# Sums of weights made by the transfers: 24 quads of a blocked fp32 kernel, and a third block carried through DRAM

## The chip, the cores and the metric

The kernel runs on one core of a Trainium2 chip. The metric is the device time of one launch in microseconds. The engines are named as in the profile: PE (TensorE matmuls), PEld (TensorE weight loads), DVE (VectorE), ACT (ScalarE), POOL (GpSimd), SP (SyncE, which issues most DMAs).

## The reference

One transformer-like layer on 256 tokens of width 2048, all in fp32: a gated feed-forward, a mixer and a second feed-forward, each behind a norm, added to the residual.

```python
def _swiglu(x, w_gate, w_up, w_down):
    return (jax.nn.silu(x @ w_gate) * (x @ w_up)) @ w_down

def _hybrid_mixer(u, w_in, ...):
    p = u @ w_in
    z_a, z_b, g_a, g_b = jnp.split(p, IN_SPLITS, axis=-1)
    y_a = _rwkv7_branch(z_a, ...) @ w_proj_a
    y_b = _pool_branch(z_b, pool_w, pool_scale) @ w_proj_b
    m = jax.nn.sigmoid(g_a) * y_a + jax.nn.sigmoid(g_b) * y_b
    return m @ w_out

h = x
f = _swiglu(_rmsnorm(h, ln_ffn1_pre), ffn1_gate, ffn1_up, ffn1_down)    # D_FF = 5632
h = h + 0.5 * _rmsnorm(f, ln_ffn1_post)
h = h + _rmsnorm(_hybrid_mixer(_rmsnorm(h, ln_mix_pre), ...), ln_mix_post)
f = _swiglu(_rmsnorm(h, ln_ffn2_pre), ffn2_gate, ffn2_up, ffn2_down)
h = h + 0.5 * _rmsnorm(f, ln_ffn2_post)
```

The RWKV branch is a recurrence over the 256 tokens in 16 heads; the pool branch takes running means. Nearly all arithmetic is in the products with the weights.

## The kernel before, in words

**Products in three passes.** A weight tile of 128 rows by 512 columns, two of them side by side, arrives in a buffer `w` (tag `w32`, five buffers of 128x1024). ScalarE copies it to a rounded type as `wH`, VectorE subtracts that from the original and gives the remainder `wL` (`split`). The activations have been split in the same way into `xH` and `xL`, transposed, so that a row block of 128 features is a stationary operand. `mm3` then issues three matmuls: high by high, high by low, low by high. A plain `pair` takes two row blocks k and k+1 for both halves of the tokens: 12 matmuls of 512 columns.

**Quads.** A `Columns` object treats two columns of 512 side by side: `f` and `l` (gate and up, or two neighbouring columns of one weight). For a quad, two row blocks k and k+1 of both columns are multiplied by a scheme with seven products in place of eight, in the manner of Strassen and Winograd. It needs sums of the activations (`sums`, kept in `sm`) and sums of the four weight tiles, made on VectorE: `t13` (128x1024: two first sums), then two further sums of 512 columns. `early` and `late` are the form in gate blocks and `quad` that in down and output columns. `join` and `merge` put the product banks together.

**Stages.** Each feed-forward has eleven gate blocks of 512 columns (`GATE1`, `GATE2`: how many quads each has; the early part of a block's quads runs inside the block before it), then `down` for the columns 0 and 1, and again for 2 and 3 (`DOWN1`, `DOWN2`: ten quads in each of the two, and where they start). The mixer's columns of `w_in` go in an order written out (`MIX_ORDER`), then come `w_proj_a` in four columns and `w_out` by `down` with three quads each time (`OUT_QUADS`: number, first, step).

**Turning blocks.** A result block [tokens, features] that feeds the next product must be transposed. There are two ways. `transpose_split` lets TensorE transpose it (four `tr` matmuls for each half of the tokens) and splits it out of PSUM. `carry` lets VectorE transpose blocks of 32x32 (`turned`, tile `T`), stores the result to DRAM (`cx<-T`) and fetches it back in four pieces in the right order (`x<-cx`). In the mixer the blocks c of the gated mix (`sga`) below `MIX_DMA` are carried, the others go through TensorE. `carry` also leaves in `raws` a way to get the block for the activation sums: here a second fetch.

**Order.** The program is recorded first. A planner (`Plan`) simulates it with costs and due times, and writes out one fixed order for each engine. For a transfer it takes bytes by `RATE` (335 bytes per ns) after 1900 ns, then `LAND` (1800 ns) and `CARRY` (1200 ns) where it depends on another transfer. Units `u` (36 buffers of 128x1024) hold everything else; spare ones are lent to `w32`, `wH` and `wL`.

Of the kernel before, what the change touches and what calls it, by code (L numbers as in the profile page):

```python
# [12 lines left out]
F32 = mybir.dt.float32  # L13
# [6 lines left out]
P = 128  # L20
# [27 lines left out]
EASE = 2.0  # L48
GATE1 = [0, 0, 3, 4, 4, 4, 4, 4, 4, 4, 4]
GATE2 = [0, 0, 3, 4, 4, 4, 4, 4, 4, 4, 4]  # L50
OUT_QUADS = ((3, 2, 1.0), (3, 1, 1.0))
DOWN1 = ((10, 1, 2.0), (10, 1, 1.3))
DOWN2 = ((10, 1, 2.0), (10, 1, 1.3))
SCRATCH = 1024
SPARE = 1
SPARE2 = 4
HOLD = 3e5
MIX_DMA = 2
Z_DMA = "l0 k0 v0 r0 k1 v1 r1"
POOL_DMA = [True, True]  # L60
MIX_ORDER = "B0 S l0 k0 p0+p1 r0 m0 m1 v0 m2 c0 B1 m3 k1 b0 b1 v1 r1 c1 B2 b2 B3 b3 A0 A1 A2 A3"
# [38 lines left out]
RATE = 335.0  # L100
LANES = 8
CARRY = 1200.0
SWITCH = 100.0
RUN = 16
COLD = 4800.0
# [6 lines left out]
KEPT = 4  # L112
# [3 lines left out]
class Plan:  # L116
# [155 lines left out]
    def deadlines(s):  # L272
        for o in s.ops:
            for p in o.preds:
                s.ops[p].succs.append(o)
        soon = {}
        for o in s.ops:
            if o.stream == "chain":
                soon[o.i] = max([soon[q] + s.ops[q].dur + SYNC for q in o.preds if q in soon
                                 and s.ops[q].nom == o.nom] or [0.0])  # L280
        idx, tip, run = {}, {}, []
        for o in s.ops:
            g = max([idx.get(q, -1) if s.ops[q].eng == "PE" else tip[q] for q in o.preds]
                    or [-1])
            tip[o.i] = g
            o.run = None
            if o.eng != "PE" or o.stream != "chain":
                continue
            idx[o.i] = len(idx)
            far = max([tip[q] for q in o.preds if s.ops[q].eng != "PE"] or [-1])  # L290
            if not run or run[-1].cfg != o.cfg or far >= idx[run[0].i] or len(run) == RUN \
                    or run[-1].psum[0].kind != o.psum[0].kind:
                run = []
            run.append(o)
            o.run = run
        for o in reversed(s.ops):
            d = o.nom + (0.0 if o.eng == "PE" else o.lag) + soon.get(o.i, 0.0) * EASE
            for x in o.succs:
                if o.eng == "PE" and x.eng == "PE":
                    continue  # L300
                e = x.dl - o.dur - SYNC - (2500 if o.nbytes else 0)
                if e < d:
                    d = e
            o.dl = d

    def simulate(s):
# [66 lines left out]
        def go(o):  # L373
# [22 lines left out]
            if o.nbytes:  # L396
                dma = max(now + 1900, dma) + o.dur
                o.end = dma + LAND
                if any(ops[q].nbytes for q in o.preds):
                    o.end += CARRY  # L400
                if e != "POOL":
                    lanes.append(o.end)
                    heapq.heappush(events, (o.end, next(rel), None))
            else:
                o.end = now + dur
# [125 lines left out]
class Block:  # L531
# [166 lines left out]
    def sums(s, x, out):  # L698

        nc = s.nc  # L700
        V = nc.vector
        fl = lambda t: t.rearrange("p a b t -> p (a b t)")
        (a11, a21), (a12, a22) = [[x[:, :, b, h] for h in range(2)] for b in range(2)]
        f = s.unit((P, 4, 2, P), F32, "sf")
        g = f if len(x.shape) < 6 else f.rearrange("p m a (i t) -> p m a i t", i=4)
        V.tensor_tensor(out=g[:, 0], in0=a21, in1=a22, op=ALU.add)
        V.tensor_tensor(out=g[:, 1], in0=g[:, 0], in1=a11, op=ALU.subtract)
        nc.scalar.mul(f[:, 0], f[:, 0], -1.0)
        V.tensor_tensor(out=g[:, 2], in0=a11, in1=a21, op=ALU.subtract)
        V.tensor_tensor(out=g[:, 3], in0=a12, in1=g[:, 1], op=ALU.subtract)  # L710
        fH, fL = [s.unit((P, 4, 2, P), F32R, n_) for n_ in ("sH", "sL")]
        s.split(fl(f), fl(fH), fl(fL))
        for i in range(2):
            out.append([(fH[:, m, i], fL[:, m, i]) for m in range(4)])
# [110 lines left out]
                in_=d.rearrange("(i s) (q c) -> q s i c", s=32, q=4)[q])  # L825
        return x

    def carry(s, T1, T, raws, j=None):
        x, d = s.carry_raw(T1)
        view = lambda t: t.rearrange("p (i a b h t) -> p a b h i t", i=4, a=2, b=2, h=2)  # L830
        if j is None:
            j = len(T)
            T.extend(s.new_T(1) if j < KEPT else [None])

        def parts():
            if T[j] is None:
                T[j], = s.new_T(1)
            H, L = [t.rearrange("p k (h c) -> p (k h) c", h=2)
                    .rearrange("p m (i t) -> p i m t", i=4) for t in T[j]]
            s.split(x.rearrange("p (i m t) -> p i m t", i=4, t=32), H, L)  # L840
        if T[j] is None:
            s.later[j] = parts
            raws.append(lambda: view(x))
        else:
            parts()
            raws.append(lambda: view(s.fetch(d, 1024, 4)))

    def sumsq(s, src, acc):
        s.nc.scalar.activation(out=s.rtmp("junk").bitcast(mybir.dt.bfloat16), in_=src,
# [17 lines left out]
class Columns:  # L867

    def __init__(s, blk, wf, cf, wl, cl, at, KT, sm, quads, bank, apart=None):
        s.b, s.wf, s.cf, s.wl, s.cl, s.at, s.KT, s.sm = blk, wf, cf, wl, cl, at, KT, sm  # L870
        s.quads, s.new, s.apart = quads, bank, apart
        n = len(quads)
        s.rest = [k for k in range(0, KT, 2) if k not in quads]
        std = KT - 2 * n
        s.left = dict(f0=std + n, f1=std, l0=std + n, l1=std + n)
        if apart:
            s.left.update(p1=n, p5=n, p6=n, p7=n)
        else:
            s.left.update(l0=std + 2 * n, f0=std + 2 * n, l1=std + 2 * n, f1=std + n)
        s.banks, s.t4 = {}, {}  # L880
# [13 lines left out]
    def pair(s, k, b):  # L894
        w, c0 = (s.wf, s.cf) if b == "f" else (s.wl, s.cl)
        for i, wH, wL in s.b.load_w(w, k, 2, c0, 512):
            for h in range(2):
                s.mul(f"{b}{h}", s.rows(i, h), (wH, wL))

    def early(s, k):  # L900
        q = s.b
        V = q.nc.vector
        va, vb = q.raw4(k, s.wf, s.cf, s.wl, s.cl)
        t13 = q.unit((P, 2, 512), F32, "t13")
        V.tensor_tensor(out=t13, in0=va, in1=vb[:, :1].to_broadcast([P, 2, 512]),
                        op=ALU.subtract)
        V.tensor_tensor(out=va[:, 1], in0=va[:, 0], in1=t13[:, 1], op=ALU.add)
        i = s.quads.index(k)
        if i % 2 == 0:
            s.t4[i] = q.unit((P, 2, 512), F32, "t4")  # L910
        V.tensor_tensor(out=s.t4[i - i % 2][:, i % 2], in0=vb[:, 1], in1=va[:, 1],
                        op=ALU.subtract)
        b11, t2 = q.halves(va)
        t1, t3 = q.halves(t13)
        S_ = s.sm[k // 2]
        end = k == s.quads[-1]
        s.mul("l0", s.rows(k, 0), b11, end)
        s.mul("f1", S_[1], t2, end)
        s.mul("f0", S_[0], t1, end)
        s.mul("l1", S_[2], t3, end)  # L920
# [14 lines left out]
    def join(s):  # L935
# [4 lines left out]
        A.copy(p5, b["f0"])  # L940
        V.tensor_tensor(out=b["f1"], in0=b["f1"], in1=u0, op=ALU.add)
        A.copy(s2, b["f1"])
        V.tensor_tensor(out=b["f0"], in0=b["f0"], in1=s2, op=ALU.add)
        V.tensor_tensor(out=b["l1"], in0=b["l1"], in1=s2, op=ALU.add)
        V.tensor_tensor(out=b["f1"], in0=b["l1"], in1=p5, op=ALU.add)

    def quad(s, k):
        q = s.b
        V = q.nc.vector
        va, vb = q.raw4(k, s.wf, s.cf, s.wl, s.cl)  # L950
        t13 = q.unit((P, 2, 512), F32, "t13")
        V.tensor_tensor(out=t13, in0=va, in1=vb[:, :1].to_broadcast([P, 2, 512]),
                        op=ALU.subtract)
        b11, b22 = q.halves(va)
        V.tensor_tensor(out=vb[:, 0], in0=va[:, 0], in1=t13[:, 1], op=ALU.add)
        t4 = q.tmp("t4")
        V.tensor_tensor(out=t4, in0=vb[:, 1], in1=vb[:, 0], op=ALU.subtract)
        t1, t3 = q.halves(t13)
        t2, b21 = q.halves(vb)
        h4 = q.unit((P, 2, 512), F32R, "h4")  # L960
# [12 lines left out]
    def merge(s):  # L973
# [4 lines left out]
        A.copy(u[0], b["p1"])  # L978
        add(u[1], b["p6"], u[0])
        add(u[2], b["p7"], u[1])  # L980
        add(u[1], b["p5"], u[1])
        add(u[3], b["p5"], u[2])
        s.u = dict(l0=u[0], l1=u[2], f0=u[1], f1=u[3])

    def plus(s, c):
# [6 lines left out]
class Kernel(Block):  # L992
# [31 lines left out]
    def ffn(s, wg, wu, wd, uT, rs, gpost, resid, emit, reload, quads, downs, xs=None):  # L1024
# [39 lines left out]
        for b in range(1, nb):  # L1064
            jobs[b] = Columns(s, wg, b * 512, wu, b * 512, s.T_at(nT) if b > 1 else at, NKD,
                              su, [2 * i for i in range(quads[b])],
                              s.psum if b % 2 else s.bank)
        for b in range(1, nb):
            J = jobs[b]
            while s.after and b == 3:  # L1070
# [6 lines left out]
        def late_T(k):  # L1077
            if hT[k // 4] is None:
                s.later[k // 4]()
            return at_h(k)  # L1080
        s.down(wd, late_T, NKF, s.post(gpost, 0.5, resid, emit, reload, xs is None), raws,
               downs, 4 * KEPT)

    def spread(s, rs, out):
        for h in range(2):
# [25 lines left out]
                s.sums(x.rearrange("p (a b) (h t) -> p a b h t", a=2, h=2), su)  # L1111
        return nT

    def down(s, wd, at, KT, ev, raws, plan, q0=0):
        sm = {}
        for c, (nq, first, step) in ((0, plan[0]), (2, plan[1])):
            J = Columns(s, wd, c * 512, wd, c * 512 + 512, at, KT, sm,
                        [q0 + 2 * i for i in range(nq)], s.bank, s.psum)
            quads = list(J.quads)
            tail = J.rest[-min(TRAIL, KT - 2 * nq) // 2:] if c else []  # L1120

            def col(b):
# [285 lines left out]
    def mixer(s, prm, uT, rs, resid, emit, gpost, reload):  # L1408
# [125 lines left out]
        sx = []  # L1534

        def sums_x():
            for i in range(MIX_SUMS):
                x = s.unit((P, 4, S), F32, "sx")
                uH, uL = [t.rearrange("p k t -> p (k t)").bitcast(F32) for t in uT[i]]
# [60 lines left out]
        for c in range(4):  # L1600
            s.gemm_tok(prm["w_proj_a"], c * 512, at_a, NKW, ev_pa(c))
        s.plan.lend = "O" in MIX_LEND
        s.down(prm["w_out"], s.T_at(mT), NKD, s.post(gpost, 1.0, resid, emit, reload), raws,
               OUT_QUADS)
        s.plan.lend = False

    def pool_window(s, win, zs, mxT):
# [538 lines left out]
```

## Time and profile before

| what | value |
|---|---|
| median of 3 runs | 1989.6 us (1989.53 to 1990.06) |
| profiled execution | 1989.87 us, span 1988.0 us |
| busy PE / PEld / DVE / ACT / POOL | 1976.1 / 1631.9 / 1837.8 / 1220.2 / 84.4 us |
| matmuls | 9700 |
| granted TensorE clock | 0.999 in the mean of the span |
| transfers | 484.30 MB, of which GpSimd's queue 9.44 MB |

The span runs from the first to the last instruction of the profiled execution; its own time is 1.87 us longer. A row of a group reads: line, engine, operation, output<-inputs by tile name, shape, count, then busy us and mean ns of one, then the idle time of the engine before it with what ended it. All recorded operations share one source line, so they are told apart by tile names. `t<-w,w` is a weight sum, `wL<-w,wH` a remainder of plain weights, `wL<-t,wH` that of a sum. A PE is called busy from the start of a matmul to its modelled end, and matmuls overlap.

### The profile page before, as it was taken

What the parts mean: (1) busy time and instruction counts of PE and PEld (TensorE: products, weight loads), DVE (VectorE), ACT (ScalarE), POOL (GpSimd) and SP (SyncE); (2) the same over time, 40 slices, a digit from 0 to 9 for tenths busy, and PEclk for the clock granted to TensorE, in tenths of its full rate; (3) what the DMA queues carried; (4) which work ended last, traced back from release to release, by engine and by line L of the source; (5) the groups of instructions that cost most, each with busy time, mean ns of one, the idle gap of its engine ahead of it and who ended that gap; (6) DMA issues with size and microseconds to landing.
All of it is one profiled execution on the core that took longest, in us unless ns stands there. A gap on an engine that the chain in (4) does not pass through costs nothing.

```text
span 1988.0 us, 28260 instructions
## 1 busy us (share of the span) xinstructions
PE 1976.1 (99%) x9700; PEld 1631.9 (82%) x9700; DVE 1837.8 (92%) x2327; ACT 1220.2 (61%) x1571; POOL 84.4 (4%) x142
## 2 busy tenths in 40 slices
PE   9999999999999999999999999999999999999998
PEld 7888888888888888888888788878888888888886
DVE  7999999999999988998899789998999999999996
ACT  8665666566656667864664455575655666666563
POOL 0000000000000120001300100010000000000000
PEclk9999999999999999999999999999999999999999
DMA  8968788786667788758666499577788887766674
GB/s 316 320 224 298 260 279 294 252 269 209 213 204 259 242 263 276 217 167 247 180 192 190 129 321 293 190 274 228 260 276 291 279 284 242 269 213 216 201 259 147
DMA packets 268063, 484.30 MB, mean 244 GB/s; under 512 B 23952, under 2 KB 52880, under 8 KB 267920
## 3 DMA queue, kind: packets, MB, share of 16 engines
q1 hardware_dynamic: 264256, 472.66, 72.7%
q0 software_dynamic: 3232, 9.44, 1.4%
q8 instruction: 76, 1.25, 0.3%
q14 instruction: 67, 0.55, 0.1%
q10 hardware_dynamic: 432, 0.40, 0.1%
HBM read 454.76 MB, written 26.61 MB: 242 GB/s over the span
## 4 chain that ended last, share of the span: by engine, by line
PE 94%; DVE 2%; ACT 1%; DMA 1%; issue 1%; SPq 0%; POOLq 0%; ACTq 0%; DVEq 0%
PE l L517 34%; PE f L517 30%; PE mm L517 21%; PE p L517 6%; DVE wL L517 1%; DMA w<-in_ffn_gate_dram 1%; DMA w<-in_w_in_dram 1%; PE pY L517 0%; ACT wH L517 0%; PE pA L517 0%; PE tr L517 0%; PE pU L517 0%; DVE AR L517 0%; PE pSa L517 0%; DVE BK L517 0%
## 5 line engine op out<-in xcount | busy, mean ns | idle before, releaser
L517 ACT CAST wH<-w 128x1024 fp32r<-128x1024 f32 (+1 forms) x712 | 727.5, 1043 | 489.2 <-PE f L517 124.8
L517 DVE TENSOR_TENSOR wL<-w,wH 128x1024 fp32r<-128x1024 f32 (+1 forms) x712 | 849.7, 1209 | 77.6 <-ACT wH L517 57.9
L517 PE MATMUL l<-wL,xH 128*128 128x512 f32 x828 | 322.2, 389 | 1.0 <-DVE wL L517 1.0
L517 PE MATMUL l<-wH,xH 128*128 128x512 f32 x828 | 322.2, 389 | 0.0
L517 PE MATMUL l<-wH,xL 128*128 128x512 f32 x828 | 322.1, 389 | 0.0
L517 PE MATMUL f<-wL,xH 128*128 128x512 f32 x608 | 236.6, 389 | 0.0
L517 PE MATMUL f<-wH,xH 128*128 128x512 f32 x608 | 236.6, 389 | 0.0
L517 PE MATMUL f<-wH,xL 128*128 128x512 f32 x608 | 236.5, 389 | 0.0
L517 PE MATMUL mm<-wL,xH 128*128 128x512 f32 (+1 forms) x568 | 220.0, 387 | 1.4 <-DVE wL L517 1.4
L517 PE MATMUL mm<-wH,xH 128*128 128x512 f32 (+1 forms) x568 | 220.8, 389 | 0.4 <-ACT xH L517 0.4
L517 PE MATMUL mm<-wH,xL 128*128 128x512 f32 (+1 forms) x568 | 219.3, 386 | 0.0
L517 ACT CAST wH<-t 128x1024 fp32r<-128x1024 f32 (+1 forms) x158 | 165.3, 1046 | 84.2 <-DVE t L517 27.8
L517 DVE TENSOR_TENSOR wL<-t,wH 128x1024 fp32r<-128x1024 f32 (+1 forms) x158 | 191.4, 1211 | 9.2 <-PE f L517 4.0
L517 DVE TENSOR_TENSOR t<-w,w 128x1024 f32<-128x1024 f32 (+1 forms) x194 | 195.6, 1016 | 3.6 <-DMA w<-in_ffn_down_dram 1.8
L517 PEld LDWEIGHTS l<-wL,xH 128*128 128x128 f32 x828 | 155.5, 188 | 33.4 <-DVE wL L517 1.3
L517 PEld LDWEIGHTS l<-wH,xH 128*128 128x128 f32 x828 | 155.5, 188 | 32.4 <-ACT wH L517 0.2
L517 PEld LDWEIGHTS l<-wH,xL 128*128 128x128 f32 x828 | 155.4, 188 | 32.2
L517 PEld LDWEIGHTS f<-wL,xH 128*128 128x128 f32 x608 | 114.2, 188 | 23.6
L517 PEld LDWEIGHTS f<-wH,xH 128*128 128x128 f32 x608 | 114.1, 188 | 23.7
L517 PEld LDWEIGHTS f<-wH,xL 128*128 128x128 f32 x608 | 114.1, 188 | 23.6
L517 PEld LDWEIGHTS mm<-wL,xH 128*128 128x128 f32 x568 | 106.7, 188 | 23.1 <-DVE wL L517 2.7
L517 PEld LDWEIGHTS mm<-wH,xH 128*128 128x128 f32 x568 | 106.7, 188 | 22.2 <-ACT xH L517 0.8
(318 smaller groups left out, 2832.9 us busy)
## 6 DMA issues: line engine op xcount, KB each, us to landing
w<-in_w_in_dram SPq DMA_DIRECT2D x120, 512.0 KB, 4.2
w<-in_ffn_gate_dram SPq DMA_DIRECT2D x218, 256.0 KB, 4.9
w<-in_ffn_up_dram SPq DMA_DIRECT2D x106, 512.0 KB, 5.4
w<-in_ffn_up_dram SPq DMA_DIRECT2D x210, 256.0 KB, 5.1
w<-in_ffn_gate_dram SPq DMA_DIRECT2D x102, 512.0 KB, 5.9
w<-in_ffn_down_dram SPq DMA_DIRECT2D x96, 512.0 KB, 4.6
w<-in_ffn_down_dram SPq DMA_DIRECT2D x160, 256.0 KB, 3.8
x<-cx SPq DMA_DIRECT2D x136, 128.0 KB, 5.4
```

What stands on the lines that cost most here:

```text
L517: ins = o.fn(*[real(x) for x in o.a], **{n: real(x) for n, x in o.k.items()})
```

## The change

- **Accumulating transfers.** In chosen quads (`s.dma`) the tile `t13` is no longer computed on VectorE. SP loads the tile f of row block k into both halves of `t13`. GpSimd's queue then issues two transfers from DRAM that add (`accum_op=ALU.add`): tile l of row block k onto the first half, tile f of row block k+1 onto the second. The other three tiles of the quad come by SP as before. The chosen quads: number 3 of every gate block that has four (`GATE_ACC`), and numbers 6 and 8 of each of the two column pairs of the down product (`DOWN_ACC`). That is 2 x (8 + 4) = 24 of the kernel's 120.
- **Signs.** A transfer can only add here, so the scheme's signs are turned: `t13` becomes a sum for all quads, and the sums of activations, the second weight sums and the final additions change between add and subtract accordingly. One ScalarE negation in `sums` goes.
- **Third mixed block.** `MIX_DMA` goes from 2 to 3: block 2 of the mix is carried through DRAM too. In the mixer `carry` keeps the fetched tile for the sums, and the second fetch goes (`keep`).
- **Output quads.** They take the row blocks 6, 8, 10 in place of 0, 2, 4 (`OUT_FROM`), and in the first column pair they begin after the fourth plain pair, not after the second.
- **Planner.** An accumulating transfer is costed 3000 ns more (`ADDING`), and its due time moves ahead by `ADDING + CARRY`.

```diff
-OUT_QUADS = ((3, 2, 1.0), (3, 1, 1.0))
+OUT_QUADS = ((3, 4, 1.0), (3, 1, 1.0))
...
+DOWN_ACC = 6, 8
+GATE_ACC = 3,
...
-MIX_DMA = 2
+MIX_DMA = 3
+OUT_FROM = 6
...
+ADDING = 3000.0
...
                 e = x.dl - o.dur - SYNC - (2500 if o.nbytes else 0)
+                if "accum_op" in o.k:
+                    e -= ADDING + CARRY
...
                     o.end += CARRY
+                if "accum_op" in o.k:
+                    o.end += ADDING
...
-        V.tensor_tensor(out=g[:, 0], in0=a21, in1=a22, op=ALU.add)
+        V.tensor_tensor(out=g[:, 0], in0=a21, in1=a22, op=ALU.subtract)
         V.tensor_tensor(out=g[:, 1], in0=g[:, 0], in1=a11, op=ALU.subtract)
-        nc.scalar.mul(f[:, 0], f[:, 0], -1.0)
         V.tensor_tensor(out=g[:, 2], in0=a11, in1=a21, op=ALU.subtract)
-        V.tensor_tensor(out=g[:, 3], in0=a12, in1=g[:, 1], op=ALU.subtract)
+        V.tensor_tensor(out=g[:, 3], in0=a12, in1=g[:, 1], op=ALU.add)
...
-    def carry(s, T1, T, raws, j=None):
+    def carry(s, T1, T, raws, j=None, keep=True):
...
-            T.extend(s.new_T(1) if j < KEPT else [None])
+            keep = j >= KEPT
+            T.extend([None] if keep else s.new_T(1))
...
         if T[j] is None:
             s.later[j] = parts
-            raws.append(lambda: view(x))
         else:
             parts()
-            raws.append(lambda: view(s.fetch(d, 1024, 4)))
+        raws.append(lambda: view(x if keep else s.fetch(d, 1024, 4)))
...
+    def four(s, k):
+        q = s.b
+        t13 = q.unit((P, 2, 512), F32, "t13")
+        if k not in s.dma:
+            va, vb = q.raw4(k, s.wf, s.cf, s.wl, s.cl)
+            q.nc.vector.tensor_tensor(out=t13, in0=va,
+                                      in1=vb[:, :1].to_broadcast([P, 2, 512]), op=ALU.add)
+            return va, vb, t13
+        get = lambda k, f: (s.wf if f else s.wl)[k * P:k * P + P,
+                                                 (s.cf if f else s.cl):][:, :512]
+        for i in range(2):
+            q.nc.sync.dma_start(out=t13[:, i], in_=get(k, 1))
+        va, vb = [q.raw().rearrange("p (a c) -> p a c", a=2) for _ in range(2)]
+        q.nc.sync.dma_start(out=va[:, 0], in_=get(k, 0))
+        q.nc.sync.dma_start(out=va[:, 1], in_=get(k + 1, 1))
+        q.nc.sync.dma_start(out=vb[:, 1], in_=get(k + 1, 0))
+        for i in range(2):
+            q.nc.gpsimd.dma_start(out=t13[:, i], in_=get(k + i, i), accum_op=ALU.add)
+        return va, vb, t13
...
     def early(s, k):
...
-        va, vb = q.raw4(k, s.wf, s.cf, s.wl, s.cl)
-        t13 = q.unit((P, 2, 512), F32, "t13")
-        V.tensor_tensor(out=t13, in0=va, in1=vb[:, :1].to_broadcast([P, 2, 512]),
-                        op=ALU.subtract)
+        va, vb, t13 = s.four(k)
         V.tensor_tensor(out=va[:, 1], in0=va[:, 0], in1=t13[:, 1], op=ALU.add)
...
         V.tensor_tensor(out=s.t4[i - i % 2][:, i % 2], in0=vb[:, 1], in1=va[:, 1],
-                        op=ALU.subtract)
+                        op=ALU.add)
...
+            jobs[b].dma = [2 * i for i in GATE_ACC if i < quads[b]]
...
-               downs, 4 * KEPT)
+               downs, 4 * KEPT, DOWN_ACC)
...
-    def down(s, wd, at, KT, ev, raws, plan, q0=0):
+    def down(s, wd, at, KT, ev, raws, plan, q0=0, acc=()):
...
+            J.dma = [quads[i] for i in acc if i < nq]
...
         s.down(prm["w_out"], s.T_at(mT), NKD, s.post(gpost, 1.0, resid, emit, reload), raws,
-               OUT_QUADS)
+               OUT_QUADS, OUT_FROM)
```

The same replacement of the first sum by `four` stands in `quad`; `join` and `merge` change the signs of two additions each.

More of the change, by code (lines that the diff above doesn't have):

```diff
@@ L870, in __init__ @@
         s.b, s.wf, s.cf, s.wl, s.cl, s.at, s.KT, s.sm = blk, wf, cf, wl, cl, at, KT, sm
+        s.dma = ()
         s.quads, s.new, s.apart = quads, bank, apart
@@ L942, in join @@
         A.copy(s2, b["f1"])
-        V.tensor_tensor(out=b["f0"], in0=b["f0"], in1=s2, op=ALU.add)
+        V.tensor_tensor(out=b["f0"], in0=b["f0"], in1=s2, op=ALU.subtract)
         V.tensor_tensor(out=b["l1"], in0=b["l1"], in1=s2, op=ALU.add)
-        V.tensor_tensor(out=b["f1"], in0=b["l1"], in1=p5, op=ALU.add)
+        V.tensor_tensor(out=b["f1"], in0=p5, in1=b["l1"], op=ALU.subtract)
     def quad(s, k):
@@ L949, in quad @@
         V = q.nc.vector
[L950 to L953, printed above, removed]
+        va, vb, t13 = s.four(k)
         b11, b22 = q.halves(va)
@@ L956, in quad @@
         t4 = q.tmp("t4")
-        V.tensor_tensor(out=t4, in0=vb[:, 1], in1=vb[:, 0], op=ALU.subtract)
+        V.tensor_tensor(out=t4, in0=vb[:, 1], in1=vb[:, 0], op=ALU.add)
         t1, t3 = q.halves(t13)
@@ L980, in merge @@
         add(u[2], b["p7"], u[1])
-        add(u[1], b["p5"], u[1])
-        add(u[3], b["p5"], u[2])
+        for o, x in ((u[1], u[1]), (u[3], u[2])):
+            V.tensor_tensor(out=o, in0=b["p5"], in1=x, op=ALU.subtract)
         s.u = dict(l0=u[0], l1=u[2], f0=u[1], f1=u[3])
@@ L1536, in sums_x @@
         def sums_x():
+            sx.clear()
             for i in range(MIX_SUMS):
```

## The prediction

> **What bounds the kernel now.** I read the page first, then the span cut by stage, then the chain in one gate block, then the table of waits. The page has three engines that look full or nearly so, and the bytes moved:
>
> ```profile
> PE 1976.1 (99%) x9700; PEld 1631.9 (82%) x9700; DVE 1837.8 (92%) x2327; ACT 1220.2 (61%) x1571; POOL 84.4 (4%) x142
> DMA packets 268063, 484.30 MB, mean 244 GB/s; under 512 B 23952, under 2 KB 52880, under 8 KB 267920
> ```
>
> The span cut at the stage borders (columns: engine busy us and instructions, granted clock, DMA share, GB/s):
>
> ```profile
> 0.00:18.00 18.00, 15.56 (x65) 12.31 (x65) 10.23 (x19) 12.41 (x24) 0.75 (x7) 1.00 0.88 291
> 18.00:650.00 632.00, 631.71 (x2789) 523.06 (x2790) 609.62 (x652) 399.42 (x454) 6.85 (x29) 1.00 0.78 260
> 650.00:1320.00 670.00, 666.97 (x3934) 549.65 (x3933) 596.43 (x991) 413.27 (x656) 75.70 (x104) 1.00 0.72 224
> 1320.00:1975.00 655.00, 655.00 (x2892) 542.53 (x2891) 618.64 (x663) 393.41 (x436) 0.56 (x1) 1.00 0.75 249
> 1975.00:1988.00 13.00, 6.83 (x26) 4.35 (x24) 2.89 (x5) 1.68 (x4) 0.54 (x1) 0.87 0.31 108
> ```
>
> The second and fourth rows are the two feed-forward stages, and PE is the first column of each. A busy PE need not be a PE at its peak, so I check it by the pace of its matmuls, in the chain between 215 and 230 us (start us, length us, what):
>
> ```profile
> 217.78 11.56 PE l L517 x51
> ```
>
> 51 matmuls in 11.56 us are 0.2267 us each. The 2789 matmuls of the second row at that pace are 632.2 us in a window of 632.0, and the 2892 of the fourth 655.5 us in 655.0: every matmul of both stages starts one pace after the last, at a granted clock of 1.00. There the time is the number of matmuls, and nothing else can shorten it. What PE waits for in the whole span is short (us in total, times, longest):
>
> ```profile
> PE mm L517 <- DVE wL L517: 2.1, 4, 0.7
> ...
> PE l L517 <- DVE wL L517: 1.0, 1, 1.0
> ```
>
> So VectorE costs PE 2.1 + 1.0 = 3.1 us by this table, although VectorE itself is busy 92%. The gaps of PE lie in the first, third and last rows of the cut: 2.4, 3.0 and 6.2 us.
>
> **The change part by part.** First the matmuls, since they set the time. The lists of quads per gate block, per down column and per output column keep their lengths, and a quad issues the same products before and after; only the signs of the sums differ. The output quads move from rows 0, 2, 4 to 6, 8, 10: still three in each pair of columns. PE loses one thing: the third mixed block is no longer turned by TensorE. Two of the four `sga` groups go, 8 of these 16 transposes; around 1202 us the chain holds the two of that block:
>
> ```profile
> L517 PE MATMUL tr<-ident,sga x16: 270/272/273, 1201.5 to 1213.6; 128*128 128x128 f32 x16
> ...
> 1201.67 0.44 PE tr L517 x4
> ...
> 1202.34 0.44 PE tr L517 x4
> ```
>
> Two groups by 0.44 us are 0.88 us, on the path: **-0.9 us**.
>
> Second, VectorE. The first sum of a quad is one pass over 1024 columns:
>
> ```profile
> L517 DVE TENSOR_TENSOR t<-w,w 128x1024 f32<-128x1024 f32 x120 | 146.2, 1219 | 3.1 <-DMA w<-in_ffn_down_dram 1.8 <-DMA w<-in_w_in_dram 1.3
> ...
> 219.85 1.22 DVE L517 TENSOR_TENSOR t<-w,w 128x1024 f32<-128x1024 f32 x1
> 220.99 0.69 DVE L517 TENSOR_TENSOR l<-l,s 128x512 f32<-128x512 f32 x1
> ```
>
> The next instruction starts 1.14 us after it, so 24 of the 120 leave 27.4 us of VectorE's queue: 16 in gate blocks (one in each of the blocks with four quads, eight per feed-forward), 8 in the down stages. All of it lies where PE keeps its pace, so it is worth **0**. The cover is PE itself; it would be gone only if PE ran out of work there. Signs cost nothing, being other operations of the same instructions. The 18 calls that make the activation sums each lose one negation on ScalarE (0.42 us in the row below): 7.6 us on an engine that is busy 61% and waits for PE's buffers: **0**.
>
> ```profile
> 1215.74 0.42 ACT L517 ACTIVATE sf<-sf 128x256 f32<-128x256 f32 x1 [0.24 <-DVE sf L517]
> L517 DVE TENSOR_TENSOR sL<-sf,sH 128x1024 fp32r<-128x1024 f32 x18 | 21.9, 1220 | 0.3 <-ACT sH L517 0.3
> ACT wH L517 <- PE f L517: 149.4, 113, 5.8
> ```
>
> Third, transfers. An accumulating quad had four loads of 256 KB from SP; it has five from SP and two from GpSimd's queue. That is 24 x 3 x 0.262 = 18.9 MB more on 484.3, some 0.79 MB in each gate block of 40.8 us, or 19 GB/s. The gate block with most traffic shows what is bearable:
>
> ```profile
> 1383.00:1424.00 41.00, 41.00 (x183) 33.96 (x182) 38.16 (x41) 25.73 (x29) 0.00 (x0) 1.00 0.96 327
> 1506.00:1547.00 41.00, 41.00 (x183) 33.96 (x182) 40.55 (x43) 24.83 (x28) 0.00 (x0) 1.00 0.87 305
> SPq L517 <- DVE wL L517: 778.0, 400, 10.8
> ```
>
> At 327 GB/s PE is busy 41.00 of 41.00 us. The next fullest would go from 305 to 324. SP waits 778 us for buffers that VectorE frees, so loads are limited by room and not by the channel, and 24 more issues fit in there: **0**. In the mixer SP saves transfers: two carried blocks fetched twice were 2 x 9, three fetched once are 3 x 5.
>
> Fourth, the new wait. The first sum is ready only when an accumulation has landed, and it starts only when the first loads have. On GpSimd's queue nothing urgent stands behind: the gate windows above show it idle (0.00, x0), and in the second feed-forward its next work after the down quads is the last norm at 1970.82 us, some 30 us later (an estimate: a dozen plain pairs of 12 matmuls follow, at 2.7 us each). On VectorE the waiting instruction is the 512-wide addition that takes the accumulated sum, and behind it in the queue stand the weight remainders (`wL`) on which PE lives. No row shows an accumulation, so I bound its landing:
>
> ```profile
> w<-in_ffn_down_dram SPq DMA_DIRECT2D x96, 512.0 KB, 4.6
> w<-in_ffn_down_dram SPq DMA_DIRECT2D x160, 256.0 KB, 3.8
> hsp<-fg POOLq DMA_DIRECT2D x16, 256.0 KB, 4.2
> msp<-sgb POOLq DMA_DIRECT2D x8, 256.0 KB, 5.4
> w<-in_rwkv_g_dram POOLq DMA_DIRECT2D x2, 256.0 KB, 5.5
> ...
> 679.93 0.56 POOL L517 TENSOR_TENSOR rs<-rt,mhalf 128x1 f32<-128x1 f32 x1 [50.58 <-DVE rt L517]
> 703.42 7.26 POOL L517 TENSOR_TENSOR rs<-rt,mhalf 128x1 f32<-128x1 f32 x1 [9.07 <-DVE rt L517]
> L517 POOL DMA_DIRECT2D hsp<-fg x16 | 9.0, 567 | 4.2 <-ACT junk L517 2.2 <-PE tr L517 2.0
> ```
>
> Low end 4.2 us, a plain store from GpSimd; high end two passes of 5.4 and one stall of GpSimd as long as its worst row, 10.8 + 7.3 = 18 us. I take the nearest row, a GpSimd load of 256 KB at 5.5, and add 0.8 for twice the bytes (4.6 against 3.8): an estimate of 6.3 us. The order of instructions is fixed by the kernel's planner, whose constants give an accumulation 1900 + 782 + LAND 1800 + CARRY 1200 + ADDING 3000 = 8.7 us. So at 6.3 the sum is there before VectorE comes to it: **0**. If it lands later, VectorE stands still. It has some room: eight gate blocks, the first and last here, leave it 0.42 to 2.71 us idle of 40.80,
>
> ```profile
> 100.00:140.80 40.80, 40.80 (x182) 33.80 (x181) 40.38 (x44) 28.27 (x33) 0.00 (x0) 1.00 0.77 253
> 385.60:426.40 40.80, 40.80 (x182) 33.80 (x181) 38.09 (x40) 26.00 (x30) 0.00 (x0) 1.00 0.84 277
> ```
>
> in the mean of the eight 1.2, and the change adds 1.1. So PE notices an accumulation from about 8.7 + 1.2 + 1.1 = 11 us on.
>
> Here the Trainium skill speaks against the change: SBUF — State Buffer, Who interferes with whom, says that a VectorE operation with two SBUF inputs contends with GpSimd's reads of SBUF, and blames starved descriptor generation when a GpSimd-issued transfer is late, though it infers that two-input operations spare that generation. The trace agrees for the reads, by the two rows of the same small power above, 0.56 and 7.26 us. By the harsher reading the sum would be that of case (a) below, by the milder one the forecast.
>
> Fifth, the mixed block now goes through VectorE and DRAM. VectorE gets one transpose of 1.24 us and loses 0.16 us at the split; PE needs the block late: the output stage starts at 1210.6 us on four plain pairs (12 x 0.2267 = 2.7 us each), one quad and another pair, so rows 8 to 11 are due about 17 us after it and about 27 us after the block's last addition (near 1201.5 us).
>
> ```profile
> 1200.25 1.29 DVE L517 TENSOR_TENSOR sga<-sga,mb 128x512 f32<-128x512 f32 x2
> L517 DVE STREAM_TRANSPOSE T<-sg 128x1024 f32<-128x1024 f32 x22 | 27.3, 1240 | 0.1
> cx<-T SPq DMA_DIRECT2D x32, 512.0 KB, 3.5
> x<-cx SPq DMA_DIRECT2D x136, 128.0 KB, 5.4
> 1210.61 0.39 PE L517 MATMUL f<-wH,xH 128*128 128x512 f32 x1
> 1214.08 1.29 DVE L517 TENSOR_TENSOR xL<-tr,xH 128x512 fp32r<-128x512 f32 x2
> ```
>
> Transpose, store and fetch are 1.2 + 3.5 + 5.4 = 10 us, the split and sums some 5: hidden with about 10 us to spare. Tighter is the last block, still turned by TensorE: its pair comes fourth in the new order, 8.2 us after 1210.6, so at 1218.8, where the old order put three pairs and two quads before it. It is ready at 1215.4, so 3.4 us are left. I take 0; the other end is a stall of 3 us if VectorE's extra 1.1 us and the reordered sums land in front of it.
>
> The sum: 0.88 us off the profiled execution, 1989.87 - 0.88 = 1989.0. That execution stands 0.27 above the median of the runs, 1989.6, so the forecast for a median is **1988.7**.
>
> **The rivals.** (a) Accumulations late, slower. If one takes over 11 us, VectorE's room in each gate block is used up, its `wL` come late and PE loses the excess in each of the 16 gate quads. At 12 us: 16 x 1 = 16 us, 2005. The bound of 0.2% is passed at 11.3. For it speak the 7.26 us above and that VectorE is at 99% in some blocks; against it that GpSimd issues a transfer in 0.567 us in the mean of the 16 above, and that its load landed after 5.5. (b) PE's waits on VectorE go, faster: 0.9 + 3.1 = 4.0, 1985.6. Against it: those waits lie at the stage borders and in the mixer, where no accumulating quad is. (c) PE has unseen room, faster. PE's weight loads fill 33.80 of 40.80 us, 83%; if the rest were room that VectorE's 27.4 us opened one for one, 1989.6 - 0.9 - 27.4 = 1961. The pace of 0.2267 us without a gap speaks against it. The Trainium skill, Perfetto Trace Analysis, Identifying the Most-Contended Engine, says that headroom of TensorE is to be judged by that share and not by matmul busy time; by that rule there would be room, and the trace disagrees. (d) The output stage waits for its fourth pair: up to +3, 1991.7, still inside 0.2%.
>
> **How the numbers follow.** This kernel's measurements tell a change of about 0.2%, 4 us, from none. Forecast, with (d) as its upper edge: 0.76, its own range 1986.5 to 1992, the lower edge for half of the waits of (b). (a): 0.16. (b) reaching beyond 0.2%: 0.06. (c): 0.02. The forecast case is the same within 0.2%: 0.76; slower 0.16; faster 0.08. For 8 in 10 the range goes from 1986, which leaves out (c) and part of (b), to 1996, which takes in the mild part of (a), accumulations near 11.5 us.
>
> **What would show it.** Right: PE's instruction count down by 8 and the pace in both feed-forward stages unbroken; VectorE busy down by about 28 us less 1; 18.9 MB more moved; 16 accumulations from GpSimd in the gate stages landing under 9 us. Wrong: rows in which `w<-w,t` on VectorE waits for the accumulated tile for several us in each gate block, with PE waits on `wL` behind them, would be (a); PE waits before the fourth pair of the output stage would be (d); gaps gone in the mixer would be (b).

## The result, and the profile after

| kernel | median | before beside it | ratio, 95% interval |
|---|---|---|---|
| changed | 1985.78 us (1985.29 to 1987.15, 22 runs) | 1989.43 | 0.9982 [0.9976, 0.9988] |

The change takes 3.65 us off, four times the 0.9 us forecast, and the interval puts it between 2.4 and 4.8 us. The median lies 0.2 us below the lower end of the range for 8 in 10, which was 1986 to 1996. The profiled execution of the changed kernel took 1987.15 us (span 1985.4), the slowest of the 22, so its trace accounts for 2.7 us of the 3.65, against 1989.87 of the profiled execution before.

Engines and bytes on the page of the changed kernel, and its queues:

```profile
PE 1974.6 (99%) x9692; PEld 1630.8 (82%) x9692; DVE 1813.0 (91%) x2303; ACT 1210.7 (61%) x1552; POOL 118.8 (6%) x190
DMA packets 278000, 503.19 MB, mean 253 GB/s; under 512 B 25056, under 2 KB 53472, under 8 KB 277856
q1 hardware_dynamic: 267280, 478.96, 73.6%
q0 software_dynamic: 10144, 22.03, 5.3%
```

There are 8 matmuls fewer, VectorE is 24.8 us less busy, and 18.9 MB more are moved. The span cut at the same borders (the fifth row is left out, as it ends elsewhere):

```profile
0.00:18.00 18.00, 15.57 (x65) 12.34 (x65) 10.23 (x20) 12.40 (x24) 0.75 (x7) 1.00 0.90 293
18.00:650.00 632.00, 631.86 (x2789) 522.88 (x2790) 594.19 (x639) 395.72 (x446) 28.16 (x53) 1.00 0.85 274
650.00:1320.00 670.00, 668.04 (x3938) 551.18 (x3937) 601.60 (x996) 413.21 (x653) 67.94 (x104) 1.00 0.73 227
1320.00:1975.00 655.00, 655.00 (x2891) 542.35 (x2891) 604.08 (x647) 387.69 (x427) 21.44 (x25) 1.00 0.81 262
```

Read the counts behind PE. Until 650 us both kernels have issued the same 65 + 2789 matmuls: the first feed-forward gained nothing, with VectorE 15 us less busy in it. Between 650 and 1320 us the changed kernel issued 3938, the one before 3934, of which 8 were the dropped transposes. So it is 12 matmuls further on, 12 x 0.2267 = 2.7 us, all of it won in the mixer and at its two borders. The second feed-forward again adds nothing.

What PE waits for between 600 and 800 us and between 1180 and 1320 us, first in the kernel before (two rows), then in the changed one (one row for the first stretch and none for the second):

```profile
PE l L517 <- DVE wL L517: 1.0, 1, 1.0
PE mm L517 <- ACT xH L517: 0.6, 1, 0.6
```

```profile
PE tr L525 <- DVE fg L525: 0.5, 1, 0.5
```

The first gap was near 750 us, in the mixed quads, the second near 1305 us, before the second feed-forward. Both are gone. The one row of the changed kernel is a new wait near 683 us, where the norm's result `fg` is transposed ahead of the mixer. The waits understate what PE loses. Taken by the starts of its matmuls, as the excess over their usual spacing, the loss falls from 1.4 to 0.1 us between 745 and 760 us and from 1.6 to 0.5 us between 1285 and 1312 us, and it rises from 0.1 to 0.8 us between 670 and 690 us. The chain of work says the same of the second border. Before, ScalarE's work stood in it; after, PE alone:

```profile
1303.18 0.94 ACT xH L517 x4
...
1304.45 0.91 ACT xH L517 x3
1305.36 0.61 ACT junk L517 x2
```

```profile
1297.67 0.44 PE tr L525 x4
...
1301.09 6.00 PE mm L525 x26
```

### The profile page after: what moved, and what is told of

It reads as the page before. It is cut to its first block, busy times and chain, and to the rows that moved or that the text cites. A ratio compares the mean times of both kernels' runs of the same rounds, so it can differ in the third digit from the quotient of the medians.

```text
span 1985.4 us, 28410 instructions
## 1 busy us (share of the span) xinstructions
PE 1974.6 (99%) x9692; PEld 1630.8 (82%) x9692; DVE 1813.0 (91%) x2303; ACT 1210.7 (61%) x1552; POOL 118.8 (6%) x190
## 3 DMA queue, kind: packets, MB, share of 16 engines
q1 hardware_dynamic: 267280, 478.96, 73.6%
q0 software_dynamic: 10144, 22.03, 5.3%
## 4 chain that ended last, share of the span: by engine, by line
PE 94%; DVE 3%; DMA 1%; ACT 1%; issue 1%; SPq 0%; POOLq 0%; ACTq 0%; DVEq 0%
PE l L525 33%; PE f L525 30%; PE mm L525 22%; PE p L525 6%; DVE wL L525 1%; DMA w<-in_ffn_gate_dram 1%; PE pY L525 0%; PE pA L525 0%; ACT wH L525 0%; PE tr L525 0%; PE pU L525 0%; DMA w<-in_ffn_down_dram 0%; DVE AR L525 0%; DMA w<-in_w_in_dram 0%; PE pSa L525 0%
## 5 line engine op out<-in xcount | busy, mean ns | idle before, releaser
L525 DVE TENSOR_TENSOR t<-w,w 128x1024 f32<-128x1024 f32 (+1 forms) x170 | 167.2, 988 | 7.5 <-DMA w<-in_ffn_down_dram 5.6
```

The source lines that it names most:

```text
L525: ins = o.fn(*[real(x) for x in o.a], **{n: real(x) for n, x in o.k.items()})
```

## The experiments

Twelve kernels, all edits of the changed kernel. Each ratio is to the kernel before on the same chip in the same session, whose median stands beside it.

| kernel | median | before | ratio, 95% interval |
|---|---|---|---|
| e1_acc_only | 1989.62 | 1989.77 | 0.9999 [0.9991, 1.0008] |
| e2_carry_only | 1987.72 | 1989.77 | 0.9989 [0.9980, 0.9997] |
| e3_signs_only | 1990.33 | 1989.77 | 1.0003 [0.9994, 1.0012] |
| e4_adding_4000 | 1986.57 | 1989.77 | 0.9983 [0.9975, 0.9992] |
| e5_adding_minus | 1986.81 | 1989.75 | 0.9985 [0.9976, 0.9994] |
| e6_two_per_block | 1986.64 | 1989.75 | 0.9984 [0.9975, 0.9993] |
| e9_carry_old_quads | 1995.99 | 1989.75 | 1.0032 [1.0020, 1.0044] |
| e10_g2_later | 1987.75 | 1989.75 | 0.9990 [0.9981, 0.9999] |
| e11_g2_waits | 1986.76 | 1989.45 | 0.9985 [0.9976, 0.9994] |
| e7_gate_acc_only | 1987.68 | 1989.45 | 0.9990 [0.9981, 0.9999] |
| e8_down_acc_only | 1986.16 | 1989.45 | 0.9984 [0.9975, 0.9993] |
| e12_early_out_quads | 1988.19 | 1989.45 | 0.9993 [0.9984, 1.0002] |

The intervals are about 0.09% wide to each side, 1.8 us, so a difference of 1 us between two kernels is read from the traces, not from the medians.

### The two halves, and an order that differs without work

```diff
 e1_acc_only          MIX_DMA = 2, OUT_FROM = 0, OUT_QUADS = ((3, 2, 1.0), (3, 1, 1.0))
 e2_carry_only        DOWN_ACC = (), GATE_ACC = ()
 e3_signs_only        both of these
 e4_adding_4000       ADDING = 4000.0
```

**e1_acc_only.** 

> The changed kernel with its third block turned by TensorE again (MIX_DMA 2, OUT_FROM 0, output quads from the second pair): accumulations and signs alone. Theory A (gaps at the two stage borders, each with its own cause): the gap near 749 us goes, that near 1303 us stays, 16 sga transposes: about 0.6 us under the kernel before, 1988.8. Theory B (VectorE's 27 us of room pays wherever it lies): most of the gain is here, about 2.7 us under before, 1986.7. Theory C (any new order of the planner moves the border gaps by a microsecond either way): anywhere within 1.5 us of before, with the 749 us gap not tied to the accumulations.

**e2_carry_only.** 

> The changed kernel with GATE_ACC and DOWN_ACC empty: the carried third block, the moved output quads and the signs, no accumulation. Theory A: 0.9 us of transposes and the 1.0 us gap near 1303 us go, the gap near 749 us stays: about 1.9 under before, 1987.5. Theory B: 0.9 under before, 1988.5, and the gap near 1303 us stays. Theory C: 0.9 under before, give or take 1.5.

**e3_signs_only.** 

> Neither accumulations nor the third carried block: only the signs, the missing negation and the single fetch of the carried mix blocks differ from before. Theories A and B: the time of before within 0.3 us, 1989.4, with both border gaps as before (1.4 us near 749, 1.0 near 1303). Theory C: gaps of another size in other places, up to 1.5 us either way.

**e4_adding_4000.** 

> The changed kernel with ADDING 4000 in place of 3000: the same work, accumulations ordered 1 us earlier by the planner. Theories A and B: the time of the changed kernel within 0.3 us, 1985.8, borders as in its trace. Theory C: a difference of 0.5 to 1.5 us from the changed kernel, located at the stage borders, although no work differs.

PE's waits in the two stretches, for e1_acc_only (nothing in the first; three rows in the second), e2_carry_only (one row in the first; nothing in the second) and e3_signs_only (one and three rows):

```profile
PE mm L525 <- DVE xL L525: 0.7, 2, 0.4
PE mm L525 <- DVE rt L525: 0.5, 1, 0.5
PE tr L525 <- DVE fg L525: 0.3, 1, 0.3
```

```profile
PE l L525 <- DVE wL L525: 1.0, 1, 1.0
```

```profile
PE l L525 <- DVE wL L525: 0.7, 1, 0.7
PE mm L525 <- DVE xL L525: 0.7, 2, 0.4
```

e4_adding_4000 has none in either. So the gaps go one by one: the accumulations take the first, the third block with the moved quads the second. Theory B falls: with all 27 us of VectorE's room, e1 lies 0.15 us under the kernel before and 0.7 us under e3, which differs from it by the accumulations alone; that is about the size of the first gap. Theory A holds for the places, though e1 and e3 have a second border that is worse than in the kernel before (1.5 us of waits against 0.6), which hides what e1 wins at the first; that much of theory C is true. e3 missed what theories A and B expected of it: its gaps are not those of the kernel before. e4 does the work of the changed kernel in another order and has the same time within the intervals, with both gaps gone.

### Which accumulations, and how they reach the first gap

The 16 gate accumulations and the 8 of the down stages were tried apart:

```diff
 e7_gate_acc_only     DOWN_ACC = ()
 e8_down_acc_only     GATE_ACC = ()
```

**e7_gate_acc_only.** 

> The changed kernel without the 8 accumulations of the down stages. Theory D (an order that the planner finds after the down stage lets the g2 loads go 1.3 us earlier): either outcome near 748 us; 1985.8 without the gap, 1987 with it. Theory E: VectorE's room in the down stage, the last before the border, is what counts: the gap stays, 1987.

**e8_down_acc_only.** 

> The changed kernel without the 16 accumulations of the gate stages, with the 8 of the down stages. Theory E: the gap near 748 us is gone as in the changed kernel, 1985.8. Theory D: either outcome, and where the gap is gone the g2 loads start near 714.0 us and not 715.3.

By the medians e8 alone has the gain of the whole change, and e7 no more than e2, which has no accumulation. By the traces e8 has no wait at the first gap, and e7 has a small rest of it, where e2 has 1.0 us:

```profile
PE l L525 <- DVE wL L525: 0.2, 1, 0.2
```

Here is what lies behind the first gap, in the kernel before: VectorE's first sum of a mixed quad waits for a weight tile, whose load is the first of the two SP issues shown (issued at 720.76 us, landed 5.9 us later); just before them GpSimd issues five loads of `g2`, 512 KB for the recurrence.

```profile
717.23 1.58 POOL L517 DMA_DIRECT2D w<-in_rwkv_g_dram  x3 [0.43 <-DVE wL L517]
718.97 0.99 POOL L517 DMA_DIRECT2D w<-in_rwkv_g_dram  x2 [0.16 <-issue]
720.76 0.81 SPq L517 DMA_DIRECT2D w<-in_w_in_dram  x2
726.80 1.23 DVE L517 TENSOR_TENSOR t<-w,w 128x1024 f32<-128x1024 f32 x1 [1.30 <-DMA w<-in_w_in_dram]
```

From there VectorE works on, with three waits of 0.5 to 0.7 us for ScalarE and no other, until PE stands still for its `wL` 25 us later. The same in e8_down_acc_only:

```profile
715.53 2.57 POOL L525 DMA_DIRECT2D w<-in_rwkv_g_dram  x5
719.79 0.81 SPq L525 DMA_DIRECT2D w<-in_w_in_dram  x2
724.50 1.22 DVE L525 TENSOR_TENSOR t<-w,w 128x1024 f32<-128x1024 f32 x1
```

and in e7_gate_acc_only:

```profile
718.27 2.74 POOL L525 DMA_DIRECT2D w<-in_rwkv_g_dram  x5 [1.23 <-DVE w L525]
721.42 0.80 SPq L525 DMA_DIRECT2D w<-in_w_in_dram  x2
726.53 1.23 DVE L525 TENSOR_TENSOR t<-w,w 128x1024 f32<-128x1024 f32 x1 [0.37 <-DMA w<-in_w_in_dram]
```

The `g2` issues end 0.8 us before SP's pair in the kernel before (719.96 to 720.76), 0.4 in e7, 1.7 in e8 and in the changed kernel. This splits the kernels, e11 below apart, in two. In the seven whose down stages accumulate, GpSimd issues these loads without a wait, they end 1.7 us before the pair, and the tile lands 4.2 to 5.0 us after its issue. In the six others (the kernel before, e2, e3, e7, e9, e10) GpSimd first waits 0.4 to 1.2 us for VectorE (the brackets), the loads end 0.3 to 0.8 us before the pair, and the tile takes 5.0 to 5.9 us. PE's wait follows the lateness of this one tile through all of them: VectorE waits for it 1.3 us in the kernel before and e2, 0.8 to 0.9 in e3, e9 and e10, 0.4 in e6 and e7, and not at all in the rest; PE then waits 1.0 us, 0.6 to 0.7, 0.2, and not at all. e6 has all the accumulations and still has 0.2 us of it. Two kernels, edits of e2_carry_only, whose first gap is whole, tested the loads as the cause (excerpts; e10 also keeps that last addition under the name `joined`):

```diff
 e10_g2_later: only the planner puts the loads after the last addition of J.join
-        gH, gL = s.split_w(fill_g)
+        with s.set(behind=None if hf else s.joined):
+            gH, gL = s.split_w(fill_g)
 e11_g2_waits: GpSimd itself waits for a late result of VectorE ahead of the loads
+        late = None if hf else G.tensor_copy(s.small(1, "gw", bufs=1), lz[3][:, :1].bitcast(F32))
+        with s.set(behind=late):
+            gH, gL = s.split_w(fill_g)
```

**e10_g2_later.** 

> The kernel with the carried block and no accumulation (e2_carry_only, 1987.72 beside 1989.77 of before), with one edit: GpSimd's five loads of the gate matrix g2 for the first half of the heads wait for the last addition that joins the first mixed quads. Theory D (the gap near 748 us comes from these loads sharing the DMA engines with the quad's own weight tile, which then lands after 5.9 us and not 4.3): the tile lands 1 to 1.6 us sooner, VectorE no longer waits for it, the 1.5 us gap goes with no accumulation in the kernel: about 1986.3 (1.4 under e2_carry_only). Theory E (the accumulations took the gap away by the room that they leave on VectorE): the gap stays, 1987.7.

**e11_g2_waits.** 

> The kernel with the carried block and no accumulation (e2_carry_only, 1987.72 beside 1989.77), with GpSimd's loads of g2 for the first half of the heads put behind a copy of one column by GpSimd that needs a result of VectorE near 748 us, so that they really wait (in e10_g2_later only the planner's order changed, and they ran at 716.6 to 718.7 us as before). Theory D (these loads share the DMA engines with the weight tile of the mixed quad near 719 us): that tile lands in about 4.4 us and not 5.2 to 5.9, VectorE does not wait for it, the gap near 748 us goes though no accumulation is in the kernel: about 1986.4. Theory E (VectorE's room took the gap away): the gap of 1.0 to 1.5 us stays, 1987.7.

e10 did not do what it was meant to: the edit moves an entry in the plan, but GpSimd's queue kept its order and got no new wait, and the loads still went out just ahead of SP's pair (718.05 to 720.61 us in the trace, not the 716.6 to 718.7 of e11's expectation). The tile was late by 0.8 us, and a part of the gap is left:

```profile
PE l L525 <- DVE wL L525: 0.6, 1, 0.6
```

In e11 they go out 33 us later than in e2,

```profile
721.27 0.80 SPq L525 DMA_DIRECT2D w<-in_w_in_dram  x2
725.94 1.22 DVE L525 TENSOR_TENSOR t<-w,w 128x1024 f32<-128x1024 f32 x1
750.23 2.57 POOL L525 DMA_DIRECT2D w<-in_rwkv_g_dram  x5 [0.28 <-issue]
```

The tile lands 3.2 us after its issue, VectorE does not wait, PE has no wait between 600 and 800 us, and no accumulation is in the kernel. Theory D holds: the loads of `g2` beside it make the tile late. The median is 0.6 us better against the kernel before than e2's, less than the 1.3 expected, but inside the intervals. What the down accumulations change is thus not a load on VectorE in the place where PE waited, but when the loads of `g2` go out after the stage: 1.2 us sooner in e8 than in e2, where GpSimd waits 0.9 us for VectorE. That the planner gives them another buffer is the likely reason and is not shown; the plan was not followed back.

### What the moved output quads do

```diff
 e9_carry_old_quads   GATE_ACC = (), DOWN_ACC = (), OUT_FROM = 0, OUT_QUADS = ((3, 2, 1.0), (3, 1, 1.0))
 e12_early_out_quads  OUT_QUADS = ((3, 2, 1.0), (3, 1, 1.0))
```

**e9_carry_old_quads.** 

> No accumulations, third block carried, but the output quads at rows 0, 2, 4 as before. The plain pairs of rows 8 to 11 then stand second and third, due about 3 to 6 us after the output stage starts, while the carried block is ready no sooner than 12.5 us after its last addition. Theory (the moved quads are what hides the carried block): a PE gap of 1 to 5 us near 1213 us, and the time at or above that of before, 1989 to 1993. Rival (the transposes are all): 0.9 under before, no such gap.

**e12_early_out_quads.** 

> The changed kernel with the first column pair's output quads from the second plain pair on (OUT_QUADS 3, 2), on rows 6, 8, 10 as in the change. Theory F (the gaps before the second feed-forward go because the norm's work on VectorE and ScalarE comes earlier once the output stage has fewer late splits, whatever the quads' start in the first pair): no gap over 0.4 us between 1285 and 1310 us, 1985.8, or some more if rows 8 to 11 are now late by a microsecond near 1223 us. Rival (the later start is what clears it): 1 to 2 us of gaps there again, 1987 to 1988.

PE's waits between 1190 and 1320 us, e9 first (between 1180 and 1320), then e12:

```profile
PE f L525 <- ACT xH L525: 4.3, 1, 4.3
PE f L525 <- DVE xL L525: 0.8, 1, 0.8
```

```profile
PE f L525 <- DVE sL L525: 1.3, 1, 1.3
PE tr L525 <- DVE sga L525: 0.9, 1, 0.9
```

With the quads at rows 0, 2, 4 and their early start, PE needs the carried block at 1212.5 us. Its last piece lands at 1214.0, ScalarE has its rounded copy made at 1216.8, behind another copy, and PE has 5.1 us of waits. By the medians' differences to before (+6.2 against -2.0) e9 takes 8.3 us more than e2_carry_only, and 3 us more than was expected of it. Most of what the waits leave open is clock: right behind the longest wait, from 1216.8 to 1222.3 us, the granted clock is 0.50 in e9, and PE's matmuls start some 0.43 us apart. So the carried block pays only with the moved quads. Part of e9's loss may belong to the early start, since the later start of the first pair saves the 2.2 us of waits that e12 has. In e12 the second border is clear too, as theory F expected, so it is not the later start that clears it. Whether the carried block or the moved rows do so stays open: in e9, which has the one without the other, PE comes to that border 8 us later than in e2, and a chain that PE is late for cannot hold it up.

### Where accumulations would hurt

```diff
 e5_adding_minus      ADDING = -3000.0
 e6_two_per_block     GATE_ACC = 2, 3
```

**e5_adding_minus.** 

> The changed kernel with ADDING -3000: the planner believes that an accumulation takes 2.7 us, where the trace shows 5.2 to 6.8 us from issue to landing, so VectorE comes to the sum some 3 to 4 us too early in each of the 24 quads. If VectorE's idle room alone covers lateness (case (a) of the prediction): room of 2.3 us in a gate block, so PE loses 1 to 2 us in each of 16 blocks: 2002 to 2018. If the ring of weights that is ready ahead of PE covers it as well: VectorE waits show, PE keeps its pace in the gate blocks, and the time is that of the changed kernel, 1985.8, give or take 1.5.

**e6_two_per_block.** 

> The changed kernel with GATE_ACC 2, 3: 34 accumulating gate quads in place of 16. The DMA share of a gate block rose by 0.09 for one such quad (0.81 to 0.90 in the mean of the eight blocks), so it comes to about 1.0. Theory: VectorE's room pays nothing where PE keeps its pace: no gain; 1985.8 if the transfers still fit, 5 to 30 us slower if they are the new limit, with weight tiles late in the gate blocks. Rival (VectorE's room pays): 1984 or less.

The first gate window of each, and the fullest of e6:

```profile
100.00:140.80 40.80, 40.80 (x182) 33.78 (x181) 40.24 (x43) 27.14 (x31) 3.36 (x6) 1.00 0.88 280
```

```profile
100.00:140.80 40.80, 40.80 (x181) 33.80 (x180) 39.13 (x42) 27.98 (x32) 3.27 (x8) 1.00 1.01 323
344.80:385.60 40.80, 40.80 (x181) 33.80 (x180) 39.04 (x41) 25.68 (x29) 5.15 (x6) 1.00 1.02 322
```

PE is busy 40.80 of 40.80 us in all of them. e5 missed its aim: no row of VectorE's waits names an accumulated tile (two of the additions that take a sum waited, 1.0 us together, for a plain weight tile), so the sums were not late even with the planner 3 to 4 us too hopeful, and what lateness costs was not measured. e6 has 34 accumulating quads in the gate blocks in place of 16, frees VectorE further and fills the transfer engines, and neither moves the time: 1986.64 against 1986.57 and 1986.81 for the other variants. More accumulations per block were not tried.

## Why the prediction was wrong

- **Matmuls, -0.9 us.** Right. The count fell by 8, and the stretch from 18 to 650 us has 2789 matmuls in both kernels.
- **VectorE's room in the gate blocks, 0.** Right, and the least obvious step: e1 gains no more than the first gap over e3, e7 by its median no more than e2, e6 no more than the changed kernel, and PE is busy 40.80 of 40.80 us in each of the eight blocks. Of case (c) nothing is left: PE's weight loads still fill 33.78 of 40.80 us, and with VectorE 0.7 to 4.3 us idle in each block of the changed kernel there is no more work in them. The Trainium skill, Perfetto Trace Analysis, Identifying the Most-Contended Engine, judges TensorE's headroom by the share of weight loads and by the FLOPs done against the peak; by the share the other 17% would be room, and the trace does not agree.
- **Landing of an accumulation, estimated at 6.3 us.** Right in the median; the slowest took 9.6 us, where the prediction's sign was under 9, and nothing waited for it. The issues in the gate stages have, in the changed kernel (KB each, median us to landing):

```profile
t<-in_ffn_gate_dram POOLq DMA_DIRECT2D x16, 256.0 KB, 5.2
t<-in_ffn_up_dram POOLq DMA_DIRECT2D x16, 256.0 KB, 6.8
```

  Case (a) did not come. The harsher reading of the Trainium skill's page SBUF — State Buffer, Who interferes with whom, that VectorE starves GpSimd's descriptors, is not borne out here: a GpSimd issue of an accumulation took 0.88 to 1.08 us in the mean and 1.27 at most, more than the 0.567 of a store, but none was held for long.
- **The mixed block, 0 with 10 us to spare; the fourth pair, 0 to 3.** Right for the block in its new place: no PE wait there. Case (d) did not come either. What the prediction did not ask is what the old order would have cost: e9, with the old rows and the early start, has 5.1 us of waits, and e12, with the early start alone, 2.2.
- **The borders: the step that failed.** The prediction had the table with the waits, priced their end in case (b) at 1985.6, and gave it 0.06 beyond 0.2%, with half of those waits in the forecast's lower edge, because "those waits lie at the stage borders and in the mixer, where no accumulating quad is". So it put the waits at the borders down as untouched, worth 0 in the sum, and that failed: it looked at where the accumulations stand and not at what the waits hang on. The first wait was the end of a chain that began 25 us earlier with a weight tile late by 1.3 us, and that lateness came from transfers of another queue, whose start moved with the stage before (e11 shows the transfers as the cause). The second stood behind ScalarE's work, and it went with the third block and the moved quads (e2 against e3); which of the two did it, and through what, stays open. The waits that stand in a stage that the change does not touch at all did stay: PE on `wL` in the tile `mm` went from 2.1 to 1.9 us. So case (b) came near the measured time by luck: of its 3.1 us of waits on VectorE only 1.2 went, and the wait at the second border is one on ScalarE (1.0 us in the whole span before, 0.5 after), which the prediction did not list.
- **The sum, mis-sized.** Forecast 0.9; in the traces 2.7. By the starts of the matmuls the first border gives 1.2 us and the second 1.1, the transposes are counted at 0.9, and 0.7 is lost again near 683 us, together 2.5. The median fell by a further 0.9, which the one trace, of the slowest execution, does not show. Its loss near 683 us stands in none of the other traces, so most of the 0.9 may be that; one trace cannot show it.

## What to carry to other kernels

Where an engine is full, only what stands on its path counts: accumulations that free VectorE in full stages gain nothing there, and 8 transposes are counted at 0.9 us. For the rest, follow each remaining wait of that engine back to its first late transfer before calling it untouched: in a kernel with one planned order an edit upstream can move a transfer by a microsecond, and a chain with little slack carries most of that microsecond to the end, as the 1.3 us of the late tile became 1.0 us of wait here. A block that is moved to a slower road needs its consumer moved with it: without accumulations, the kernel with the carried block in the old order took 6 us more than the kernel before, in the new order 2 less.

## What the runs showed of the hardware

Accumulating packets hold the transfer engines about twice as long per byte as plain loads. GpSimd's queue went from 9.44 MB at 1.4% of the engines' time to 22.03 MB at 5.3%: 12.6 MB more for 3.9%, 0.31% per MB, where SP's queue has 478.96 MB at 73.6%, 0.15% per MB, as GpSimd's own transfers had before. So 6% more bytes per us (273 to 290 GB/s in the mean of the eight gate blocks) made their mean DMA share rise by 0.09, from 0.81 to 0.90. That share, which the profile works out from packet times, reached 1.02 in a stretch in which PE lost nothing.

A weight tile of 256 KB, issued by SP into a busy stretch, landed 3.2 us later with none of GpSimd's 512 KB beside it (e11), 4.2 to 5.0 us later where GpSimd's issues had ended 1.7 us before, and 5.0 to 5.9 us later where they had ended 0.3 to 0.8 us before. In e9, after a wait of 4.3 us, PE's granted clock was 0.50 from 1216.8 to 1222.3 us, and 1.00 from there on.
